# RWKV-7 mixer: the inverses of the 16x16 diagonal blocks by rows on GpSimd in place of doubling blocks on VectorE

## The chip, the cores and the metric

One core of a Trainium2 chip runs the whole program. The metric is the device time of one execution in microseconds (us), as the median of several runs. In the profile PE is the matrix engine, PEld its weight loads, DVE the vector engine, ACT the scalar engine, POOL the GpSimd engine, and SP the engine whose queue issues most DMAs.

## The reference, cut to what matters

A block of a streaming encoder: RMS norm, one input projection, two mixers side by side (a Mamba-2 state space mixer and an RWKV-7 mixer), an output projection, and a SwiGLU feed-forward layer. All is float32, 256 tokens of 2048 channels. The change lies in the RWKV-7 mixer, which the reference writes as a scan over tokens, for each of 32 heads of 64 channels:

```
def step(S, inp):
    r_t, w_t, k_t, v_t, a_t, b_t = inp
    sa = einsum('bhvk,bhk->bhv', S, a_t)
    S = S * w_t + sa[..., None] * b_t + v_t[..., None] * k_t
    return S, einsum('bhvk,bhk->bhv', S, r_t)
```

Taken by chunks of 64 tokens, the dependence of sa on earlier tokens of its own chunk is a strictly lower triangular 64x64 matrix N for each head and chunk, and the chunk needs the inverse of (I - N).

## The kernel before

**The stream.** The matrix products of the projections and of the feed-forward layer go through `gemm_a` and `gemm_b` in units: SP loads 512 KB of weights into `raw` (four buffers), ACT casts them to `whi` (L192), DVE computes the rest `wlo` (L193; four buffers each), and PE runs 24 matrix products of 256 columns (L277 to L279) or 12 of 512 (L298 to L300) on them. After each unit `side.tick()` traces the pieces of mixer work whose time has come.

**The RWKV mixer.** It is worked on in eight pairs of channel blocks, numbered 0 to 7 here: four heads and four chunks of 64 tokens each, thus 16 matrices N. A pair passes through three windows of the stream: its preparation (`PREP`), its matrices and their inverse (`AMATS`, `INV`), and the recurrence over its chunks (`CHAIN`: `step_r(c)` and `step_s(c)` for c from 0 to 3, then the group norm). So the inverse of pair k is computed in the window in which pair k-1 runs its recurrence. The numbers in the tables are ticks of a window, which has 16 of them, 12 for the first three.

**The inverse.** `amat("atb", ...)` computes N on PE and masks it on DVE. `inv_out` (L593 to L607) takes the four 16x16 diagonal blocks of each matrix out (`dg`, L602), and SP brings them over DRAM (`sc_n`, L604) into `nb` (L606), so that each of 64 partitions holds one block, `nb[i, t] = N[t, i]`. POOL sets `xb` to 64 identity matrices (L609, L610). `inv_level(s)` for s = 1, 2, 4, 8 then doubles the size of the inverted blocks in `xb`. Level 1 is a copy (L628). The others form two products for each pair of blocks, each as a DVE multiply into `pd` (L650) and a reduction (L652):

```
product(tv, n21.rearrange("p m j r -> p m r j"), x11)
product(x21, x22, tj)
```

`inv_in` (L658) transposes `xb` into `xbt` on DVE (L661), sends both over DRAM (`sc_X`, `sc_XT`, L664) back to tokens on the partitions (`cm`, L666), and spreads them into `XT` and `X` on DVE (L669). `lev16a` to `lev32b` (L686 to L723) go from 16 to 64 on PE (`ps_b`, L678). The result `XF` is first used in the next window.

**What else matters for the steps.** In the recurrence `step_s(c)` computes the new state `sn` on DVE (L766, L767), and `step_r(c+1)` reads it on PE (L736, into `ps_r`).

**Order.** Each engine works strictly through its own queue. Program order is set by the tables of ticks. The framework's scheduler then orders the instructions of each engine anew by a model of its own, except those that `keep_in_program_order` names, and sets semaphores for what depends on what. A DMA that waits in SP's queue holds up every DMA behind it.

Of the kernel before, what the change touches and what calls it, by code (L numbers as in the profile page):

```python
# [13 lines left out]
ALU = mybir.AluOpType  # L14
# [18 lines left out]
# ticks of a window at which the parts of three pairs of blocks are traced  # L33
# [8 lines left out]
class Side:  # L42
    """Work of the mixers, cut into small pieces that are traced between the pieces of the dense products."""
# [25 lines left out]
def tile_hybrid_block(ctx: ExitStack, tc: tile.TileContext, x, norm1_g, w_in, conv_w, conv_b, dt_bias, A_log, D_skip,  # L69
# [41 lines left out]
    # products that nothing reads: the tensor engine has its full clock only after a busy stretch  # L111
# [52 lines left out]
    # msk16: lower off-diagonal blocks on the way from 16 to 32 ([t, c])  # L164
# [35 lines left out]
    def square(i, pool, b, n, eng, order=lambda ins: ins):  # L200
        """the sum of squares of a quarter of each row"""
        src = h[:, b, n * 512:(n + 1) * 512]
        acc = ssq[i][:, b, n:n + 1]
        if eng == "act":
            order(nc.scalar.activation(pool.tile([P, 512], F32, name="sq_a"), src, AF.Square, accum_out=acc))
        else:
            order(nc.vector.scalar_tensor_tensor(pool.tile([P, 512], F32, name="sq_v"), src, 1.0, src, ALU.mult,
                                                 ALU.mult, accum_out=acc))
# [8 lines left out]
    def row_scale(i, pool):  # L217
        """one over the root mean square of each token, along the free dimension of every partition"""
        nonlocal R
        ps = mxt("ps_R")  # L220
        for b in range(2):
            r = finish(i, b)
            dg = pool.tile([P, P], F32, name="diag_r")
            nc.vector.tensor_scalar(dg, ident, r, None, ALU.mult)
            nc.tensor.matmul(ps[:, b * P:(b + 1) * P], ones, dg, start=True, stop=True)
        R = const.tile([P, T], F32, name="R")
        nc.scalar.copy(R, ps[:, :T])

    def scaled(ps):
        """a product of the raw rows becomes the one of the normalised rows"""  # L230
        nc.vector.tensor_tensor(ps, ps, R.unsqueeze(1).broadcast_to([P, 2, T]), ALU.mult)
        return ps

    def to_channels(n, gcol, order=lambda ins: ins):
        """a quarter of h times the norm's weight, with channels on the partitions; the rows' scale comes later"""
        nonlocal uh, ul
        if n == 0:
            uh = big.tile([P, KT, T], F32R, name="uh")
            ul = big.tile([P, KT, T], F32R, name="ul")
        tiles = []  # L240
        for k2 in range(2):
            ps = mxt("ps_n").rearrange("p (a t) -> p a t", a=2)
            tiles.append(ps)
            for b in range(2):
                for j in range(2):
                    c = n * 512 + (2 * k2 + j) * P
                    order(nc.tensor.transpose(out=ps[:, j, b * P:(b + 1) * P], in_=h[:, b, c:c + P], identity=ident))

        def half(k2):
            ks = [(4 * n + 2 * k2 + j, tiles[k2][:, j]) for j in range(2)]  # L250
            for k, ps in ks:
                order(nc.scalar.activation(uh[:, k], ps, AF.Copy, scale=gcol[:, k:k + 1]))
            for k, ps in ks:
                order(nc.vector.scalar_tensor_tensor(ul[:, k], ps, gcol[:, k:k + 1], uh[:, k].bitcast(F32), ALU.mult,
                                                     ALU.subtract))

        return half

    def load_a(w, cols, k0):
        """four row tiles of 256 columns; cols: [(place, width, column)]"""  # L260
        raw = wpool.tile([P, 4, 256], F32, name="raw", tag="raw", bufs=4)
        wv = w.rearrange("(k p) c -> p k c", p=P)
        for at, n, c in cols:
            nc.sync.dma_start(out=raw[:, :, at:at + n], in_=wv[:, k0:k0 + 4, c:c + n])
        return raw
# [17 lines left out]
    def gemm_b(w, r0, c0, acts, name):  # L283
        """acts: [(hi, lo)] with [P, T] each, one for a row tile of w; 512 columns"""
# [19 lines left out]
    def add_out(w, r0, ys, then=None):  # L304
        """ys: [(hi, lo)] of two row tiles each"""
# [9 lines left out]
    # the first product starts while x and its weights still come in, a quarter of the channels after the other  # L315
# [121 lines left out]
    def rwkv_pair(pi, st):  # L437
# [119 lines left out]
        def swap(dst, src, tmp):  # L557
            """the 64x64 blocks of src [(h c), (b c t)] transposed into dst [(h t), b c, c]"""
# [37 lines left out]
        # inverse of (I - N): blocks of 16 on one partition each, by halves of halves  # L596
        def inv_out():
# [7 lines left out]
            nb = tl("nb", (64, 272))  # L605
            nc.sync.dma_start(out=nb[:, :256].rearrange("p (i t) -> p i t", t=16),  # L606
                              in_=sc.rearrange("c (x i) t -> (c x) i t", i=16))  # L607
            xb = tl("xb", (64, 272))
# [4 lines left out]
        def inv_level(s):  # L613
            def f():
                nb, xb = st["nb"], st["xb"]
                nm = 8 // s

                def blocks(t, at, swap):
                    """block (row offset or column offset) of each of the nm diagonal blocks, [nm, s, s]"""
                    v = t[:, :nm * 34 * s].rearrange("p (m x) -> p m x", m=nm)[:, :, at:at + 16 * s]  # L620
                    v = v.rearrange("p m (j t) -> p m j t", t=16)[:, :, :, 0:s]
                    return v.rearrange("p m j t -> p m t j") if swap else v

                # nb is [i, t]: N[t, i]; xb is [t, c]
                n21 = blocks(nb, s, False)
                x11 = blocks(xb, 0, True)
                if s == 1:
                    nc.vector.tensor_copy(blocks(xb, 16, False), n21)  # L628
                    return
                x22 = blocks(xb, 17 * s, False)  # L630
                x21 = blocks(xb, 16 * s, False)
                tt = tl("tt", (64, 64), 2)
                # three free dimensions in an instruction: blocks of 2 by rows, larger ones by blocks
                if s == 2:
                    cut = [(slice(0, nm), r) for r in range(s)]
                    shp = [64, nm, s, s]
                    tv = tt[:, :nm * s * s].rearrange("p (r m c) -> p m r c", r=s, c=s)
                else:
                    cut = [(m, slice(0, s)) for m in range(nm)]
                    shp = [64, s, s, s]  # L640
                    tv = tt[:, :nm * s * s].rearrange("p (m r c) -> p m r c", r=s, c=s)
                tj = tv.rearrange("p m j c -> p m c j")

                def product(out, a, b):
                    """out[m, r, c] = sum over j of a[m, r, j] b[m, c, j]"""
                    for m, r in cut:
                        pd = tl("pd", (64, 512), 2, tag="t1")
                        pv = pd[:, :shp[1] * s * s].rearrange("p (a c j) -> p a c j", c=s, j=s)
                        bb = b[:, m] if s == 2 else b[:, m].unsqueeze(1)
                        nc.vector.tensor_tensor(pv, a[:, m, r].unsqueeze(2).broadcast_to(shp), bb.broadcast_to(shp),  # L650
                                                ALU.mult)
                        nc.vector.tensor_reduce(out[:, m, r], pv, axis=AX.X, op=ALU.add)  # L652

                product(tv, n21.rearrange("p m j r -> p m r j"), x11)
                product(x21, x22, tj)
            return f

        def inv_in():  # L658
            xbt = tl("xbt", (64, 16, 16), 2, tag="t1")
            xv = st["xb"][:, :256].rearrange("p (t c) -> p t c", c=16)  # L660
            nc.vector.tensor_copy(xbt, xv.rearrange("p t c -> p c t"))  # L661
# [12 lines left out]
        def blocks32(out, lhs, rhs, rows):  # L674
            """out[:, c] = lhs[:, c].T @ rhs[:, c] for 32x32 blocks; rows: [(input rows, output rows)]"""
            for c in range(NCH):
                for r, o in rows:
                    nc.tensor.matmul(out[o:o + 32, c], lhs[r:r + 32, c], rhs[r:r + 32, c], start=True, stop=True)  # L678
# [46 lines left out]
        # the chunks in their order  # L725
# [107 lines left out]
        inv = [inv_level(1), inv_level(2), inv_level(4), inv_level(8), inv_in, lev16a, lev16b, lev32a, lev32b]  # L833
# [239 lines left out]
    # the last 256 rows of w_down and the last norm, one half of the tokens after the other  # L1073
# [65 lines left out]
```

## Time and profile before

| what | value |
|---|---|
| time, median of 3 runs | 1697.96 us (1697.33 to 1699.16) |
| the profiled execution, from its first to its last instruction | 1697.0 us |
| PE busy | 1678.6 us, 99% |
| DVE busy | 1232.7 us, 73% |
| ACT busy | 892.1 us, 53% |
| POOL busy | 18.0 us, 1% |
| mean granted clock of PE | 0.998 |

The profile is of one execution. It gives the busy time of each engine, groups of instructions by line with their count, busy time and mean duration, the idle time ahead of them with the instruction that ended it, and a timeline with starts and durations. PE's products are pipelined: their spans overlap, so that a busy PE is not a PE at its peak. The windows of the eight pairs lie in the first 600 us, where DVE is busiest.

### The profile page before, as it was taken

The page shows a single profiled execution, that of the slowest core. Times are in us where ns is not written, and L with a number is a line of the kernel's source. Part 1 is how long each engine was busy: PE and PEld are TensorE (multiplying, and loading weights), DVE is VectorE, ACT ScalarE, POOL GpSimd, SP SyncE. Part 2 cuts the span into 40 slices and gives each one's busy share as a digit, 9 for nine tenths or more (in the row PEclk, how much of TensorE's full clock was granted, in tenths as well). Part 3 has the DMA queues.
Part 4 walks back from the last instruction along what each step waited for, and adds up shares of the span by engine and source line. Part 5 has one row for each costly group of instructions (what it writes and reads, how often), then busy time and mean ns, then how long its engine had stood idle before and what let it go on. Part 6 is the DMA issues. An engine that isn't in the chain of part 4 may idle for free.

```text
span 1697.0 us, 35291 instructions
## 1 busy us (share of the span) xinstructions
PE 1678.6 (99%) x14670; PEld 1546.5 (91%) x14670; DVE 1232.7 (73%) x1921; ACT 892.1 (53%) x1391; POOL 18.0 (1%) x57
## 2 busy tenths in 40 slices
PE   8999999999999999999999999999999999999997
PEld 8999989889898998998988999999999999999996
DVE  7998888989888868877768656556565565565657
ACT  6655665765646556666665543434434334344344
POOL 3000000000000000000000000000000000000000
PEclk9999999999999999999999999999999999999999
DMA  8554445544445456565554655555555555555553
GB/s 256 175 152 115 126 128 156 145 120 143 132 130 151 141 154 217 179 206 164 164 177 150 205 183 190 181 189 187 185 189 182 189 189 182 190 186 185 190 182 129
DMA packets 266720, 288.27 MB, mean 170 GB/s; under 512 B 43426, under 2 KB 216768, under 8 KB 265920
## 3 DMA queue, kind: packets, MB, share of 16 engines
q1 hardware_dynamic: 265232, 283.72, 54.0%
q8 instruction: 115, 1.88, 0.4%
q0 software_dynamic: 752, 1.24, 0.2%
q10 hardware_dynamic: 576, 1.05, 0.2%
q14 instruction: 45, 0.37, 0.1%
HBM read 282.27 MB, written 3.70 MB: 169 GB/s over the span
## 4 chain that ended last, share of the span: by engine, by line
PE 71%; DVE 2%; DMA 1%; ACT 1%; issue 0%; DVEq 0%
PE ps_o L298 7%; PE ps_o L300 7%; PE ps_o L299 7%; PE ps_up L279 5%; PE ps_up L277 5%; PE ps_up L278 5%; PE ps_gt L279 5%; PE ps_gt L278 5%; PE ps_gt L277 5%; PE ps_xs L277 2%; PE ps_xs L279 2%; PE ps_xs L278 2%; PE ps_z L300 2%; PE ps_z L298 2%; PE ps_z L299 2%; PE ps_bc L277 1%
## 5 line engine op out<-in xcount | busy, mean ns | idle before, releaser
L192 ACT CAST whi<-raw 128x1024 fp32r<-128x1024 f32 x508 | 532.2, 1048 | 655.2 <-PE ps_o L300 144.8
L193 DVE TENSOR_TENSOR wlo<-raw,whi 128x1024 fp32r<-128x1024 f32 x508 | 619.7, 1220 | 335.2 <-ACT whi L192 333.4
L277 PE MATMUL ps_rkv<-uh,whi 128*128 128x256 f32 x768 | 224.7, 293 | 0.0
L279 PE MATMUL ps_rkv<-uh,wlo 128*128 128x256 f32 x768 | 218.3, 284 | 0.7 <-DVE wlo L193 0.7
L278 PE MATMUL ps_rkv<-ul,whi 128*128 128x256 f32 x768 | 218.3, 284 | 0.0
L278 PE MATMUL ps_gt<-ul,whi 128*128 128x256 f32 x704 | 199.4, 283 | 0.0
L279 PE MATMUL ps_gt<-uh,wlo 128*128 128x256 f32 x704 | 199.3, 283 | 0.0
L277 PE MATMUL ps_up<-uh,whi 128*128 128x256 f32 x704 | 199.2, 283 | 0.0
L278 PE MATMUL ps_up<-ul,whi 128*128 128x256 f32 x704 | 199.2, 283 | 0.0
L279 PE MATMUL ps_up<-uh,wlo 128*128 128x256 f32 x704 | 199.2, 283 | 0.0
L277 PE MATMUL ps_gt<-uh,whi 128*128 128x256 f32 x704 | 199.2, 283 | 0.0
L277 PEld LDWEIGHTS ps_rkv<-uh,whi 128*128 128x128 f32 x768 | 146.7, 191 | 5.5 <-issue 1.4
L279 PEld LDWEIGHTS ps_rkv<-uh,wlo 128*128 128x128 f32 x768 | 146.7, 191 | 1.9 <-DVE wlo L193 1.1
L278 PEld LDWEIGHTS ps_rkv<-ul,whi 128*128 128x128 f32 x768 | 146.8, 191 | 0.6
L278 PEld LDWEIGHTS ps_gt<-ul,whi 128*128 128x128 f32 x704 | 135.1, 192 | 0.4
L277 PEld LDWEIGHTS ps_gt<-uh,whi 128*128 128x128 f32 x704 | 135.1, 192 | 0.4
L277 PEld LDWEIGHTS ps_up<-uh,whi 128*128 128x128 f32 x704 | 135.2, 192 | 0.0
L278 PEld LDWEIGHTS ps_up<-ul,whi 128*128 128x128 f32 x704 | 135.2, 192 | 0.0
L279 PEld LDWEIGHTS ps_up<-uh,wlo 128*128 128x128 f32 x704 | 135.2, 192 | 0.0
L279 PEld LDWEIGHTS ps_gt<-uh,wlo 128*128 128x128 f32 x704 | 135.1, 192 | 0.0
L298 PE MATMUL ps_o<-whi,ah 128*128 128x512 f32 x336 | 130.8, 389 | 0.0
L299 PE MATMUL ps_o<-wlo,ah 128*128 128x512 f32 x336 | 130.8, 389 | 0.0
(338 smaller groups left out, 3272.0 us busy)
## 6 DMA issues: line engine op xcount, KB each, us to landing
raw<-in_w_in_dram SPq DMA_DIRECT2D x180, 512.0 KB, 3.9
raw<-in_w_gate_dram SPq DMA_DIRECT2D x88, 512.0 KB, 3.6
raw<-in_w_up_dram SPq DMA_DIRECT2D x88, 512.0 KB, 3.5
raw<-in_w_down_dram SPq DMA_DIRECT2D x88, 512.0 KB, 3.6
raw<-in_w_out_dram SPq DMA_DIRECT2D x64, 512.0 KB, 3.9
csb<-cs_d SPq DMA_DIRECT2D x4, 1024.0 KB, 5.7
h<-in_x_dram SPq DMA_DIRECT2D x4, 512.0 KB, 7.8
g2s<-in_rwkv_g_dram SPq DMA_DIRECT2D x8, 256.0 KB, 3.3
```

The source lines that it names most:

```text
L192: order(nc.scalar.copy(hi, raw))
L193: order(nc.vector.tensor_tensor(lo, raw, hi.bitcast(F32), ALU.subtract))
L277: nc.tensor.matmul(o, wh, uh[:, kt], start=first and b == 0, stop=False)
L278: nc.tensor.matmul(o, wh, ul[:, kt], start=False, stop=False)
L279: nc.tensor.matmul(o, wl, uh[:, kt], start=False, stop=last and b == 1)
L298: nc.tensor.matmul(ps[b], ah[:, s], hi[:, k], start=first, stop=False)
L299: nc.tensor.matmul(ps[b], ah[:, s], lo[:, k], start=False, stop=False)
L300: nc.tensor.matmul(ps[b], al[:, s], hi[:, k], start=False, stop=last)
```

## The change

`inv_level` goes, and `inv_rows(i0, i1)` takes its place, four calls of four or three rows. It does forward substitution by rows: for i from 0 to 14, `N[t, i]` times row i of the inverse is added to all rows t below i. A step is a multiply into `pd` and an add into `xb`, both on GpSimd, on 64 partitions with 15 to 64 elements each; step 0 is a copy. Each step needs the one before. The transposed copy `xbt` is made on GpSimd as well, and lies in the buffer of `nb`. The ticks in `INV` stay as they are. For each pair DVE loses 22 instructions (a copy, ten multiplies, ten reductions, the transposing copy), and POOL gets 30 (two copies, 14 multiplies, 14 adds).

```diff
-            nb = tl("nb", (64, 272))
+            nb = tl("nb", (64, 256))
...
-            xb = tl("xb", (64, 272))
+            xb = tl("xb", (64, 256))
...
+        def inv_rows(i0, i1):
             def f():
+                nv = st["nb"][:, :256].rearrange("p (i t) -> p i t", t=16)
+                xv = st["xb"][:, :256].rearrange("p (t c) -> p t c", c=16)
+                for i in range(i0, i1):
+                    n, m = 15 - i, i + 1
+                    below = xv[:, m:, 0:m]
+                    if i == 0:
+                        nc.gpsimd.tensor_copy(below, nv[:, 0, 1:].unsqueeze(2))
+                        continue
+                    shp = [64, n, m]
+                    pd = tl("pd", (64, 64), 2)[:, :n * m].rearrange("p (t c) -> p t c", c=m)
+                    nc.gpsimd.tensor_tensor(pd, bc(nv[:, i, m:], m), xv[:, i, 0:m].unsqueeze(1).broadcast_to(shp),
+                                            ALU.mult)
+                    nc.gpsimd.tensor_tensor(below, below, pd, ALU.add)
             return f
...
-            xbt = tl("xbt", (64, 16, 16), 2, tag="t1")
+            xbt = tl("xbt", (64, 16, 16), tag="nb")
...
-            nc.vector.tensor_copy(xbt, xv.rearrange("p t c -> p c t"))
+            nc.gpsimd.tensor_copy(xbt, xv.rearrange("p t c -> p c t"))
...
-        inv = [inv_level(1), inv_level(2), inv_level(4), inv_level(8), inv_in, lev16a, lev16b, lev32a, lev32b]
+        inv = [inv_rows(0, 4), inv_rows(4, 8), inv_rows(8, 12), inv_rows(12, 15), inv_in, lev16a, lev16b, lev32a, lev32b]
```

The scheduler also sets other instructions in another order. Three places follow. Line numbers behind the changed function are 26 lower in the new file, and buffer numbers differ.

DVE in the window in which pair 2 is inverted, from the last state of the recurrence (`sn`) to `XT`, before:

```order
L767 TENSOR_TENSOR sn_3187<-sn_3187,pt_1153 128x128
L561 STREAM_TRANSPOSE ktt_3324<-kt_3061 128x512
L652 TENSOR_REDUCE xb_2895<-pd_3336 64x8x8
L354 SCALAR_TENSOR_TENSOR rkv_3218<-ps_rkv_2963,colA_161,rkv_3218 128x255
L661 COPY xbt_3339<-xb_2895 64x256
L193 TENSOR_TENSOR wlo_3386<-raw_3383,whi_3385 128x1024
L354 SCALAR_TENSOR_TENSOR rkv_3218<-ps_rkv_2963,colA_161,rkv_3218 128x255
L193 TENSOR_TENSOR wlo_3535<-raw_3532,whi_3534 128x1024
L560 STREAM_TRANSPOSE tmp2_3255<-rkv_3218 128x512
L746 TENSOR_TENSOR ws_3278<-ps_w_3273,nn_1898 128x128
L533 TENSOR_TENSOR ar_3727<-q_2994,pr_2785 128x8x64
L669 TENSOR_TENSOR XT_3345<-cm_3343,pmask_147 128x256
```

The same stretch of DVE's queue in the changed kernel, where L643 is `XT` and `X`, L740 and L741 are `sn`:

```order
L193 TENSOR_TENSOR wlo_3383<-raw_3380,whi_3382 128x1024
L515 TENSOR_TENSOR kt_3088<-kp_3013,pin_2806 128x512
L588 TENSOR_TENSOR atk_2946<-ps_a_3156,mask2_130 128x512
L643 TENSOR_TENSOR XT_3372<-cm_3370,pmask_147 128x256
L643 TENSOR_TENSOR X_3378<-cm_3376,pmask_147 128x256
L231 TENSOR_TENSOR ps_rkv_2981<-ps_rkv_2981,R_398 128x512
L561 STREAM_TRANSPOSE btt_3166<-bt_3086 128x512
L740 TENSOR_TENSOR sn_3213<-ps_s_3204,sn_3028 128x128
L354 SCALAR_TENSOR_TENSOR rkv_3243<-ps_rkv_2981,colA_161,rkv_3243 128x255
L741 TENSOR_TENSOR sn_3213<-sn_3213,pt_1162 128x128
L561 STREAM_TRANSPOSE ktt_3349<-kt_3088 128x512
L193 TENSOR_TENSOR wlo_3413<-raw_3410,whi_3412 128x1024
```

`XT` has moved ahead of two units' `wlo` and ahead of both `sn`. In all of pairs 2 to 7 it now stands ahead of that `sn`. PE's place for `ps_r<-sn` has not moved.

SP's queue in the same window, from the load of `nb`, before:

```order
L606 DMA nb_2893<-sc_n_2891 64x256
L290 DMA raw_3532<-in_w_out_dram 128x2x512
L290 DMA raw_3583<-in_w_out_dram 128x2x512
L290 DMA raw_3623<-in_w_out_dram 128x2x512
L664 DMA sc_X_3347<-xb_2895 64x256
L664 DMA sc_XT_3341<-xbt_3339 64x256
L290 DMA raw_3645<-in_w_out_dram 128x2x512
L666 DMA cm_3343<-sc_XT_3341 128x8x16
```

And in the changed kernel:

```order
L606 DMA nb_2911<-sc_n_2909 64x256
L290 DMA raw_3559<-in_w_out_dram 128x2x512
L638 DMA sc_X_3374<-xb_2913 64x256
L638 DMA sc_XT_3368<-xbt_3366 64x256
L290 DMA raw_3610<-in_w_out_dram 128x2x512
L640 DMA cm_3370<-sc_XT_3368 128x8x16
L640 DMA cm_3376<-sc_X_3374 128x8x16
L290 DMA raw_3650<-in_w_out_dram 128x2x512
```

`sc_X` has moved ahead of two loads of weights.

PE where pair 0's inverse is first used (`ps_b<-X`): before, in the units of `whi_1725` and `whi_1785`:

```order
L277 MATMUL ps_rkv_1506<-uh_182,whi_1725 128x256
L278 MATMUL ps_rkv_1506<-ul_183,whi_1725 128x256
L678 MATMUL ps_b_1545<-X_1498,atb_1214 32x32 x32
L279 MATMUL ps_rkv_1506<-uh_182,wlo_1726 128x256
L279 MATMUL ps_rkv_1782<-uh_182,wlo_1786 128x256
L277 MATMUL ps_rkv_1782<-uh_182,whi_1785 128x256
```

In the changed kernel:

```order
L278 MATMUL ps_rkv_1515<-ul_183,whi_1518 128x256
L279 MATMUL ps_rkv_1515<-uh_182,wlo_1519 128x256
L652 MATMUL ps_b_1554<-X_1507,atb_1214 32x32 x32
L277 MATMUL ps_rkv_1515<-uh_182,whi_1644 128x256
L278 MATMUL ps_rkv_1515<-ul_183,whi_1644 128x256
L279 MATMUL ps_rkv_1515<-uh_182,wlo_1645 128x256
```

PE meets pair 0's `X` 73 products of the stream sooner: ahead of the unit of `whi_1644`, which is `whi_1635` in the kernel before, its thirtieth unit. Pair 1's stands 31 products sooner, ahead of the forty-second unit. For pairs 2 to 7 PE has kept its order here.

More of the change, by code (lines that the diff above doesn't have):

```diff
@@ L611, in inv_out @@
             st["nb"], st["xb"] = nb, xb
-        def inv_level(s):
+        def inv_rows(i0, i1):
             def f():
[L615 to L655, printed above, removed]
```

## The prediction

> **What bounds the kernel now.** I read the page first, then PE's waits.
>
> ```profile
> PE 1678.6 (99%) x14670; PEld 1546.5 (91%) x14670; DVE 1232.7 (73%) x1921; ACT 892.1 (53%) x1391; POOL 18.0 (1%) x57
> ```
>
> ```profile
> PE ps_b L678 <- issue: 1.6, 1, 1.6
> PE ps_w L743 <- ACT rs L739: 0.8, 1, 0.8
> PE ps_b L678 <- DVE X L669: 0.7, 1, 0.7
> PE ps_rkv L279 <- DVE wlo L193: 0.7, 1, 0.7
> PE ps_b L678 <- DVE X L702: 0.4, 1, 0.4
> PE ps_b L678 <- DVE t1s L692: 0.3, 1, 0.3
> ```
>
> PE is the bound for the whole span. All that it waits for in the eight pairs' windows is these 4.5 us. So work taken off DVE can give back no more than these. Whatever makes PE wait, though, is added in full, because PE has no slack in which to catch up. Such a wait also costs something afterwards. Here are two stretches of 5 us behind the longest of the waits above; the last three columns are the granted clock of PE, the DMA share and GB/s:
>
> ```profile
> 440.00:445.00 5.00, 3.39 (x101) 2.37 (x89) 3.38 (x8) 4.00 (x11) 0.00 (x0) 0.90 0.46 130
> 445.00:450.00 5.00, 5.00 (x48) 4.19 (x48) 3.04 (x7) 4.90 (x12) 0.00 (x0) 0.76 0.00 0
> ```
>
> The clock falls to a mean of 0.90 and 0.76: 5 x 0.10 + 5 x 0.24 = 1.7 us of PE's time lost after a wait of 1.6 us.
>
> **What the change takes from DVE.** From the groups by line:
>
> ```profile
> L650 DVE TENSOR_TENSOR pd<-xb,tt 64x16 f32<-64x16 f32 (+2 forms) x40 | 14.2, 382 | 0.1
> L650 DVE TENSOR_TENSOR pd<-nb,xb 64x16 f32<-64x16 f32 (+2 forms) x40 | 13.6, 367 | 0.0
> ...
> L652 DVE TENSOR_REDUCE tt<-pd 64x8 f32<-64x16 f32 (+2 forms) x40 | 10.0, 277 | 0.2
> L652 DVE TENSOR_REDUCE xb<-pd 64x8 f32<-64x16 f32 (+2 forms) x40 | 9.8, 273 | 0.0
> ...
> L661 DVE COPY xbt<-xb 64x256 f32<-64x256 f32 x8 | 2.9, 363 | 0.0
> ...
> L628 DVE COPY xb<-nb 64x8 f32<-64x8 f32 x8 | 1.3, 160 | 2.7 <-DMA nb<-sc_n 2.7
> ```
>
> That is 51.8 us of DVE in all, 6.5 us a pair, beside PE's work. I credit the 4.5 us of waits and the 1.7 us of slow clock, 6.2 us, as the most that a lighter DVE can give.
>
> **How long there is for the new chain.** The inverse is a chain: `nb` lands, the blocks are inverted, `xbt` ends, the round trip over DRAM follows, then `XT` and `X`. Call C the time from the landing of `nb` to the end of `xbt`. DVE's timeline of pair 2 before:
>
> ```profile
> 205.63 0.17 DVE L628 COPY xb<-nb 64x8 f32<-64x8 f32 x1 [0.47 <-DMA nb<-sc_n]
> 205.72 0.68 DVE L513 TENSOR_TENSOR bt<-ta,pin 128x512 f32<-128x512 f32 x1
> ...
> 208.80 1.21 DVE L193 TENSOR_TENSOR wlo<-raw,whi 128x1024 fp32r<-128x1024 f32 x1
> ...
> 210.09 1.21 DVE L193 TENSOR_TENSOR wlo<-raw,whi 128x1024 fp32r<-128x1024 f32 x1
> ...
> 214.31 0.68 DVE L515 TENSOR_TENSOR kt<-kp,pin 128x512 f32<-128x512 f32 x1
> ...
> 216.54 1.21 DVE L193 TENSOR_TENSOR wlo<-raw,whi 128x1024 fp32r<-128x1024 f32 x1
> 217.68 0.70 DVE L561 STREAM_TRANSPOSE btt<-bt 128x512 f32<-128x512 f32 x1
> 218.31 0.24 DVE L766 TENSOR_TENSOR sn<-ps_s,sn 128x128 f32<-128x128 f32 x1
> 218.48 0.68 DVE L231 TENSOR_TENSOR ps_rkv<-ps_rkv,R 128x512 f32<-128x512 f32 x1
> 219.08 0.26 DVE L767 TENSOR_TENSOR sn<-sn,pt 128x128 f32<-128x128 f32 x1
> ...
> 220.88 0.48 DVE L354 SCALAR_TENSOR_TENSOR rkv<-ps_rkv,colA,rkv 128x255 f32<-128x255 f32 x1 [0.34 <-ACT rkv L353]
> 221.28 0.36 DVE L661 COPY xbt<-xb 64x256 f32<-64x256 f32 x1
> ...
> 227.55 0.43 DVE L669 TENSOR_TENSOR XT<-cm,pmask 128x256 f32<-128x256 f32 x1 [0.31 <-DMA cm<-sc_XT]
> 227.89 0.42 DVE L669 TENSOR_TENSOR X<-cm,pmask 128x256 f32<-128x256 f32 x1
> ```
>
> C is 16.0 us here (205.63 to 221.64), because the chain shares DVE with other work. From there to `XT` it is 5.9 us. Before the change both `sn` at 218.3 and 219.1 stand ahead of `XT`, so that the wait for `cm` keeps nobody. In the changed kernel they stand behind it: `XT`, `X`, L231, `btt`, `sn`, `rkv`, `sn`. Their durations add up to 3.2 us, and since each starts about 0.08 us ahead of its predecessor's end, they take 2.7 us. PE needs that `sn` at its old place, here for the pairs 2 and 6, with the landing for pair 6 and, in the last four rows, landing and first use for pairs 0 and 1:
>
> ```profile
> 221.39 0.28 PE L736 MATMUL ps_r<-sn,ar 64*64 64x64 f32 x4
> ...
> 482.88 0.17 DVE L628 COPY xb<-nb 64x8 f32<-64x8 f32 x1 [1.30 <-DMA nb<-sc_n]
> ...
> 497.81 0.28 PE L736 MATMUL ps_r<-sn,ar 64*64 64x64 f32 x4
> ...
> 98.45 0.16 DVE L628 COPY xb<-nb 64x8 f32<-64x8 f32 x1
> ...
> 108.87 0.28 PE L277 MATMUL ps_rkv<-uh,whi 128*128 128x256 f32 x1
> ...
> 149.61 0.12 DVE L628 COPY xb<-nb 64x8 f32<-64x8 f32 x1
> ...
> 165.71 0.28 PE L277 MATMUL ps_rkv<-uh,whi 128*128 128x256 f32 x1
> ```
>
> - Pairs 2 to 7: 221.39 - 205.63 = 15.8 us, less 5.9 and 2.7, leaves C at most 7.2 us; for pair 6, 14.9 us leaves 6.3. I take 6.75 for all six, 40.5 in all.
> - Pair 0: PE now meets `X` ahead of the unit that began at 108.87. 10.4 us, less 5.9, less 1.2 for `XT`, `rkv` and `X`, leaves 3.3.
> - Pair 1: ahead of the unit that began at 165.71. 16.1 us, less 5.9 and 0.8, leaves 9.4.
>
> Together 53.2 us. If C is the same for all pairs and above 9.4, PE waits 8C - 53.2 us more. If it is smaller, pair 1 drops out first.
>
> Behind the blocked `XT` stand also two units' `wlo` (PE uses the first some 8 us after `ps_r`, and DVE needs 2 us for it after `sn`). Behind SP's blocked `sc_X` stand loads of weights, which in the kernel before were issued some 10 us earlier but not used for 20 us. I cost both at nothing; the four buffers hide them, up to a delay of about 6 us.
>
> **How long the new chain takes.** No arithmetic runs on POOL before. The nearest rows:
>
> ```profile
> L609 POOL MEMSET xb<- 64x272 f32 x8 | 2.5, 318 | 265.6 <-DMA sc_X<-xb 265.6
> L155 POOL TENSOR_SCALAR_AFFINE_SELECT mask<-mask 64x64 f32<-64x64 f32 x4 | 1.3, 357 | 0.0
> L610 POOL MEMSET xb<- 64x16 f32 x8 | 1.0, 119 | 0.5
> ```
>
> L610 waits for L609 as each step here waits for the last: 0.5 us idle over 8, 0.06 us each. A step is then no less than 0.119 + 0.06 = 0.18 us (it also reads two operands, and has 47 elements on the mean). The nearest row that reads and writes 64x64 gives 0.357 + 0.06 = 0.42 us. I take 0.34, nearer the second, since the second also reads: 28 x 0.34 = 9.5, 0.2 for the first copy, and 0.8 for `xbt` (256 elements a partition, between 0.32 for the memset of that size and four times 0.357): 10.5 us.
>
> DVE may add to it. While the chain runs, DVE has five instructions that read two operands from SBUF: 0.68, 0.68 and three `wlo` of 1.21, 5.0 us. Whether they hold up POOL no row before can show, since POOL there only writes. I take half, 2.5. So C = 13.0 us, with bounds of 28 x 0.18 + 0.2 + 0.4 = 5.6 and 28 x 0.42 + 0.2 + 1.4 + 5.0 = 18.4.
>
> [...]
>
> **The sum.** PE waits 8 x 13.0 - 53.2 = 50.8 us more. Each of the eight waits, of 3.6 to 9.7 us, is longer than the one that cost 1.7 us of clock, so 8 x 1.7 = 13.6 us. [...] Credit: 6.2 us. Net 58.2, on the profiled 1697.0: 1755.2 us. The median of the runs shown is 0.9 us above the profiled span, so **1756 us**.
>
> **The rivals.**
>
> 1. *DVE and POOL block one another in full.* The 5.0 us then count whole: C = 15.5 and 8 x 15.5 - 53.2 = 70.8, plus 13.6, less 6.2: 1776 us. [...] Against the full price: DVE is stuck at `XT` early and then holds nothing.
> 2. *A short chain, small waits.* At 0.22 to 0.27 us a step C is near 8.5. Pair 1 does not wait; the other seven wait 7 x 8.5 - 43.8 = 15.7 us, 11.9 us of clock, less 6.2: 1719 us. For it: the memset's 0.18.
> 3. *Faster.* The one mechanism is that the chain comes off DVE's path altogether: with C up to 6.75, a step below 0.2 us, `XT` finds `cm` landed, `sn` is in time, and only pair 0 waits, 2.3 to 3.5 us, with or without 1.7 us of clock. Against that stand 6.2 us of credit, so 1694 to 1697 us. For it: before, the chain's own work on DVE is 6.5 us a pair and stretches to 16 for company; alone on POOL it has none. Against it: a step would have to run like a memset of 16 elements.
>
> **How the numbers follow.** A difference of 0.2%, 3.4 us, is about what a measurement of this kernel can tell. My forecast (C between 10 and 14.5) gets 0.60, rival 1 gets 0.22, rival 2 gets 0.12, rival 3 gets 0.06. All but the last are slower, and a little of rival 2 and half of the last are no change: slower 0.93, same 0.04, faster 0.03. The range reaches from C = 7.6 (six waits of 0.9 and one of 4.3 us, some 5 us of clock, less 6.2: 1706) to C = 18.4 (94.0 + 13.6 - 6.2 = 101, 1799, and some clock beyond one slow stretch for waits of over 10 us: 1805).
>
> **What would show it.** Right: a new wait of PE at `ps_r` (L710) for DVE's `sn` (L741), six times, each 4 to 9 us; PE waiting for DVE's `X` at `ps_b` for pairs 0 and 1; `XT` with a long idle ahead of it put down to `cm<-sc_XT`; POOL busy for 80 to 100 us more; DVE 52 us less; granted clock below 1 in the slices from 100 to 570 us. Wrong: steps of POOL under 0.2 us; PE without waits at `ps_r`; or a span that grows elsewhere, as in the feed-forward layer, which has no pairs.

## The result, and the profile after

The changed kernel takes 1787.34 us (median of 4 runs, 1784.93 to 1790.22), the kernel before in the same comparison 1697.86 us (1697.33 to 1699.16): a ratio of 1.0528, 95% interval 1.0513 to 1.0543. The forecast was 1756 us. The profiled execution spans 1788.5 us, 91.5 us more than before.

The page of the changed kernel, busy times and the row of the granted clock by slices:

```profile
PE 1708.2 (96%) x14670; PEld 1574.9 (88%) x14670; DVE 1192.5 (67%) x1745; ACT 892.0 (50%) x1391; POOL 110.4 (6%) x297
...
PEclk9989889898989989999999999999999999999999
```

POOL works 92 us more, DVE 40 us less. (DVE's 176 removed instructions add up to 51.8 us by groups, but each overlaps with its neighbours on DVE; in the trace before, DVE without them is busy 39 us less.) The clock row was all nines before; now seven of its first fifteen slices show an eight, and it is whole again from slice 16 on, where the pairs are through.

PE's waits after (total us, times, longest):

```profile
PE ps_r L710 <- DVE sn L741: 38.8, 6, 7.2
PE ps_b L652 <- DVE X L643: 15.6, 2, 10.4
PE ps_rkv L279 <- DVE wlo L193: 8.7, 4, 2.4
...
PE ps_bc L279 <- DVE wlo L193: 2.1, 1, 2.1
PE ps_b L652 <- DVE t1s L666: 1.6, 1, 1.6
```

The first two rows are the waits that were forecast, at their places and in their numbers: six at `ps_r`, two at `ps_b`, 54.4 us. The `wlo` rows are five waits that no step of the prediction had, and neither is the one for `t1s`, which follows at once on the wait for `X` at pair 1.

DVE's timeline of pair 2, and further down the place of one of those five waits:

```profile
227.38 1.23 DVE L193 TENSOR_TENSOR wlo<-raw,whi 128x1024 fp32r<-128x1024 f32 x1
...
230.46 1.23 DVE L193 TENSOR_TENSOR wlo<-raw,whi 128x1024 fp32r<-128x1024 f32 x1 [0.52 <-ACT whi L192]
...
236.57 0.68 DVE L588 TENSOR_TENSOR atk<-ps_a,mask 128x512 f32<-128x512 f32 x1
246.09 0.42 DVE L643 TENSOR_TENSOR XT<-cm,pmask 128x256 f32<-128x256 f32 x1 [8.84 <-DMA cm<-sc_XT]
...
248.62 0.28 DVE L741 TENSOR_TENSOR sn<-sn,pt 128x128 f32<-128x128 f32 x1
...
282.85 0.69 DVE L803 TENSOR_TENSOR yl<-yc,yh 128x512 fp32r<-128x512 f32 x1 [1.84 <-ACT yh L802]
283.45 0.68 DVE L534 TENSOR_TENSOR ar<-rkv,pr 128x512 f32<-128x512 f32 x1
284.06 1.22 DVE L193 TENSOR_TENSOR wlo<-raw,whi 128x1024 fp32r<-128x1024 f32 x1
```

DVE reaches `XT` at 237 and stands there 8.84 us until `cm` has landed, and the `sn` that PE wants stand behind it. Forty microseconds later DVE stands 1.84 us before `yl`, which waits for ACT's `yh`, with the next `wlo` behind it. Before the change the order at that place was `yc`, `ar`, `wlo`, `yl`, and `yl` waited for nothing:

```profile
250.55 0.68 DVE L534 TENSOR_TENSOR ar<-rkv,pr 128x512 f32<-128x512 f32 x1
251.15 1.22 DVE L193 TENSOR_TENSOR wlo<-raw,whi 128x1024 fp32r<-128x1024 f32 x1
252.30 0.69 DVE L829 TENSOR_TENSOR yl<-yc,yh 128x512 fp32r<-128x512 f32 x1
```

The scheduler has put `yl` two places earlier.

POOL's timeline of the chain of pair 2, and the groups by line that belong to it:

```profile
226.54 0.36 POOL L623 COPY xb<-nb 64x15 f32<-64x15 f32 x1 [17.95 <-DMA nb<-sc_n]
...
227.60 1.11 POOL L627 TENSOR_TENSOR pd<-nb,xb 64x39 f32<-64x39 f32 x1
...
230.54 1.29 POOL L627 TENSOR_TENSOR pd<-nb,xb 64x60 f32<-64x60 f32 x1
...
239.47 0.21 POOL L629 TENSOR_TENSOR xb<-xb,pd 64x15 f32<-64x15 f32 x1
239.74 0.61 POOL L635 COPY xbt<-xb 64x256 f32<-64x256 f32 x1
```

```profile
L627 POOL TENSOR_TENSOR pd<-nb,xb 64x28 f32<-64x28 f32 (+3 forms) x112 | 44.0, 393 | 8.8
L629 POOL TENSOR_TENSOR xb<-xb,pd 64x28 f32<-64x28 f32 (+3 forms) x112 | 39.6, 353 | 8.8
L635 POOL COPY xbt<-xb 64x256 f32<-64x256 f32 x8 | 4.9, 614 | 0.5
L623 POOL COPY xb<-nb 64x15 f32<-64x15 f32 x8 | 3.9, 489 | 216.2 <-DMA nb<-sc_n 216.2
```

A step takes 0.373 us on the mean and has 0.079 us of idle ahead (8.8 / 112). C is 28 x 0.452 + 0.49 + 0.61 = 13.8 us, and so it is in the timeline (226.5 to 240.35).

PE's windows of 5 us around that pair's wait (length, PE busy and its count, granted clock, DMA share, GB/s):

```profile
240.00:245.00 5.00, 2.43 (x23) 0.97 0.65 147
245.00:250.00 5.00, 1.04 (x13) 0.50 0.44 115
250.00:255.00 5.00, 4.92 (x27) 0.50 0.48 132
```

PE gets its data at 249 and then runs at half clock until 255. Between the first 30 us and the last microseconds the trace has 13 such stretches, 105.8 us in all. PE is idle in 31.9 of these, so (105.8 - 31.9) x 0.5 = 36.9 us of its work were lost to the clock, against 1.7 us before.

### The profile page after: what moved, and what is told of

Same layout as the page of the kernel before. It is cut to its first block, busy times and chain, and to the rows that moved or that the text cites. A ratio compares the mean times of both kernels' runs of the same rounds, so it can differ in the third digit from the quotient of the medians.

```text
span 1788.5 us, 35328 instructions
## 1 busy us (share of the span) xinstructions
PE 1708.2 (96%) x14670; PEld 1574.9 (88%) x14670; DVE 1192.5 (67%) x1745; ACT 892.0 (50%) x1391; POOL 110.4 (6%) x297
## 4 chain that ended last, share of the span: by engine, by line
PE 63%; DVE 0%; ACT 0%; DVEq 0%; issue 0%
PE ps_o L298 7%; PE ps_o L300 7%; PE ps_o L299 7%; PE ps_up L279 5%; PE ps_up L278 5%; PE ps_up L277 5%; PE ps_gt L279 5%; PE ps_gt L278 5%; PE ps_gt L277 5%; PE ps_xs L277 2%; PE ps_xs L279 2%; PE ps_xs L278 2%; PE ps_z L300 2%; PE ps_z L298 2%; PE ps_z L299 2%; PE ps_yd L928 1%
## 5 line engine op out<-in xcount | busy, mean ns | idle before, releaser
L279 PE MATMUL ps_rkv<-uh,wlo 128*128 128x256 f32 x768 | 226.6, 295 | 8.7 <-DVE wlo L193 8.7
L277 PE MATMUL ps_rkv<-uh,whi 128*128 128x256 f32 x768 | 234.8, 306 | 0.0
L278 PE MATMUL ps_rkv<-ul,whi 128*128 128x256 f32 x768 | 226.3, 295 | 0.0
L279 PEld LDWEIGHTS ps_rkv<-uh,wlo 128*128 128x128 f32 x768 | 155.8, 203 | 9.4 <-DVE wlo L193 9.2
L277 PEld LDWEIGHTS ps_rkv<-uh,whi 128*128 128x128 f32 x768 | 155.2, 202 | 6.2 <-issue 1.4
L278 PEld LDWEIGHTS ps_rkv<-ul,whi 128*128 128x128 f32 x768 | 155.9, 203 | 0.5
```

Source lines behind the costliest of these rows:

```text
L277: nc.tensor.matmul(o, wh, uh[:, kt], start=first and b == 0, stop=False)
L278: nc.tensor.matmul(o, wh, ul[:, kt], start=False, stop=False)
L279: nc.tensor.matmul(o, wl, uh[:, kt], start=False, stop=last and b == 1)
```

## The experiments

**The theory ("queue").** Nothing is wrong with the work on GpSimd itself. DVE's queue is in order, and an instruction in it that waits for the longer chain (`XT`, then `X`; 8.84 us before `XT` of pair 2) holds up what PE needs next. Each such wait then costs clock as well. **The rivals:** the work on GpSimd takes the time by blocking DVE; or the chain of many small steps is too long on any engine. With each result stand two sums from its trace: how long PE was idle from 30 us on until its last product, and what the half-clock stretches in that time cost PE beside that. (Of pin_spread's 28.8 us, 2.9 belong to a stretch at 30.5 us, ahead of the first pair's inverse.) Less the kernel before's 5.0 and 1.7, they should give the difference in span, and do within some 11%. Each ratio is to runs of the kernel before on the same chip:

| kernel | median us | ratio to before, 95% interval | PE idle | clock lost | span more than before |
|---|---|---|---|---|---|
| before | 1697.86 | 1 | 5.0 | 1.7 | 0 |
| changed | 1787.34 | 1.0528 (1.0513 to 1.0543) | 67.4 | 36.9 | 91.5 |
| pin_spread | 1768.14 | 1.0413 (1.0398 to 1.0429) | 55.3 | 28.8 | 73.0 |
| spread_late | 1759.49 | 1.0359 (1.0343 to 1.0374) | 31.0 | 40.6 | 62.1 |
| spread_pool | 1731.51 | 1.0196 (1.0170 to 1.0221) | 29.8 | 14.9 | 34.7 |
| rows7 | 1757.27 | 1.0340 (1.0325 to 1.0356) | 40.6 | 29.8 | 59.3 |
| yl_later | 1775.49 | 1.0441 (1.0422 to 1.0459) | 60.9 | 27.2 | 77.6 |
| all_moved | 1704.84 | 1.0032 (1.0021 to 1.0042) | 8.5 | 7.6 | 8.8 |
| pool_load | 1702.56 | 1.0021 (1.0012 to 1.0030) | 10.3 | 1.6 | 5.5 |
| rows_on_dve | 1712.98 | 1.0079 (1.0063 to 1.0094) | 14.6 | 8.5 | 16.2 |
| all_moved_2 | 1709.88 | 1.0082 (1.0068 to 1.0096) | 9.8 | 9.3 | 11.2 |
| clock_dose | 1786.04 (one run) | | 72.9 | 17.6 | 87.2 |
| hybrid | 1695.31 | 0.9981 (0.9972 to 0.9990) | 2.7 | 0.0 | -3.6 |

**pin_spread: only the order of `XT` and `sn`.**

```diff
-                nc.vector.tensor_tensor(dst.rearrange("p c (b t) -> p c b t", t=16),
+                pin(nc.vector.tensor_tensor(dst.rearrange("p c (b t) -> p c b t", t=16),
...
```

> Only the place of XT and X in DVE's queue changes: for the pairs 2 to 6 they move behind the two sn (they then stand 2 instructions behind the second sn, and the next unit's wlo 3 behind XT); pairs 0, 1 and 7 stay as they are. Theory 'sn': the six waits at ps_r are the whole harm of pairs 2 to 6, so five of them (33.3 us) and their clock (about 17 us) go: 1735 to 1740 us. Theory 'queue': DVE still stands before XT until cm has landed, and PE then waits about as long for the wlo that is now next behind it; 5 to 7 us each, put down to wlo and no longer to sn: 1770 to 1790 us. Theory 'POOL itself is the cost': 1787 us.

1768.14 us. PE's waits:

```profile
PE ps_y L751 <- DVE ws L720: 22.1, 5, 6.2
PE ps_b L652 <- DVE X L643: 15.7, 2, 10.2
PE ps_r L710 <- DVE sn L741: 6.1, 1, 6.1
```

The five waits for `sn` are gone, the sixth, in pair 7 where nothing moved, stays; and in place of the five PE now waits five times for `ws`, the next thing that it wants from a DVE that stands before `XT`. The theory "sn" falls. "Queue" holds, with another victim than the `wlo` that I had named, shorter waits (3.6 to 6.2 us) and a time 2 us below its range. The waits for `wlo` behind `yl` are shorter here as well (7.5 us instead of 10.8), and only the longest of them, of 1.74 us, is followed by a half-clock stretch.

**spread_late: `XT` where `cm` has landed.**

```diff
-INV = (5.002, 6.276, 7.732, 9.62, 9.939, 11.691, 11.849, 12.652, 15.9)
+INV = (5.002, 6.276, 7.732, 9.62, 9.939, 12.9, 14.1, 14.3, 15.0, 15.9)
...
+        def inv_spread():
+            for key in ("XT", "X"):
...
+                pin(nc.vector.tensor_tensor(dst.rearrange("p c (b t) -> p c b t", t=16),
...
-        inv = [..., inv_in, lev16a, lev16b, lev32a, lev32b]
+        inv = [..., inv_in, inv_spread, lev16a, lev16b, lev32a, lev32b]
```

> The spreading of cm into XT and X is traced 3 ticks (about 15 us) later and the four steps to 64 accordingly, so that DVE reaches XT after cm has landed; the chain on GpSimd stays. Theory 'queue': with C still at 13 to 14.5 us, no wait of PE of over 1 us for pairs 2 to 7, at most one for pairs 0 or 1, granted clock back at 0.99: 1690 to 1702 us. Theory 'POOL and DVE block one another' (the chain itself costs): the time stays at 1770 to 1787 us.

1759.49 us: a miss. The wait that it was made against is gone: no wait at `ps_r` is left, and `XT` of pair 2 starts at 266.54 with no idle ahead. But the steps from 16 to 64 now follow one another within half a unit, and PE waits between them. The longest of these waits, of 4.0, 4.5 and 5.4 us, lie at the pairs 0 and 1, where DVE still stands 9.8 and 7.8 us before `XT`. Waits, and windows of PE in pair 2:

```profile
PE ps_b L656 <- DVE t1s L670: 9.9, 2, 5.4
PE ps_b L656 <- DVE X L647: 9.7, 6, 4.0
```

```profile
265.00:270.00 5.00, 3.12 (x113) 1.00 0.14 33
270.00:275.00 5.00, 4.16 (x84) 0.52 0.36 93
```

Two waits of 1.15 and 0.7 us among 128 products of 32x32 come ahead of a stretch of 13.7 us at half clock, from 270.2 on; a third wait of 0.8 us and more such products lie within it. In the pairs 2 to 6 the clock cost 3.0 to 6.4 us each, more than the waits. So this run doesn't say that the chain harms; it says that my new place was bad.

**spread_pool: DVE out of the chain.**

```diff
-                nc.vector.tensor_tensor(dst.rearrange("p c (b t) -> p c b t", t=16),
+                nc.gpsimd.tensor_tensor(dst.rearrange("p c (b t) -> p c b t", t=16),
```

> XT and X are computed on GpSimd, at the old ticks, so that DVE never waits for cm. Theory 'queue': the waits of pairs 2 to 7 at ps_r (38.8 us) and at wlo (10.8 us) go; PE meets X for pairs 0 and 1 as early as in the changed kernel, so 10 and 5 us stay there and perhaps 1 us more since GpSimd is slower at it, with about 10 us of clock: 1715 to 1730 us. Theory 'POOL and DVE block one another': more work on GpSimd, so no better than 1787 us.

1731.51 us, 1.5 us above the range of "queue" and 56 us less than the changed kernel, with more work on GpSimd. PE's waits:

```profile
PE ps_b L652 <- POOL X L643: 17.3, 2, 10.9
PE ps_rkv L279 <- DVE wlo L193: 10.2, 4, 3.2
...
PE ps_bc L279 <- DVE wlo L193: 2.2, 1, 2.2
```

All waits for `sn` are gone; C is as long as ever (224.6 to 238.5 in pair 2). The rival "POOL and DVE block one another" would have had it no better than 1787 us. What I had wrong: the five waits for `wlo` stay. They have nothing to do with the wait before `XT`.

**rows7: a shorter chain, rows 0 to 6 alone.**

```diff
-                for i in range(i0, i1):
+                for i in range(i0, min(i1, 7)):
```

> Only rows 0 to 6 of the substitution are done, 12 multiplies and adds in place of 28 (rows 7 to 14 are left out, so the inverse is incomplete); XT still stands ahead of sn in DVE's queue. C should come to 5.5 to 7 us, at the edge of the 6.75 us that the pairs 2 to 7 were said to have. Theory 'queue': waits at ps_r of 0 to 0.5 us each, pair 0 still waits about 3 us, 1694 to 1706 us. Theory 'the cost goes with the work on GpSimd': 12/28 of 90 us stay, 1735 us.

1757.27 us, above the ranges of both theories: another miss. C is 7.2 us (214.7 to 221.9 in pair 2). PE's waits:

```profile
PE ps_r L710 <- DVE sn L741: 16.1, 6, 3.6
PE ps_rkv L279 <- DVE wlo L193: 9.2, 4, 3.0
PE ps_w L717 <- ACT rs L713: 5.8, 6, 1.4
```

The waits at `ps_r` fell from 6.5 to 2.7 us each, so they do follow the length of the chain. They did not fall to nearly nothing: my margin of 6.75 us is some 2 us too wide for this kernel, in which `XT` stands 7 instructions ahead of the first `sn` and not 4. The clock fell only from 36.9 to 29.8 us: what a wait costs in clock depends little on its length. And the waits for `wlo` stay here too. In pair 1, `XT` has come to stand ahead of `ws`, and PE waits 4.7 us for that `ws`: the same mechanism at one more place. Why PE also waits 5.8 us for ACT's `rs` stays open.

**yl_later: the waits for `wlo`.** DVE's order at the end of a window, with the changed kernel's rows ahead of this kernel's:

```
L798 yc<-ps_g,yc   L311 h<-ps_o,h x2   L803 yl<-yc,yh   L534 ar<-rkv,pr   L193 wlo<-raw,whi
L799 yc<-ps_g,yc   L312 h<-ps_o,h x2   L535 ar<-rkv,pr   L194 wlo<-raw,whi   (yl further down)
```

```diff
-            nc.vector.tensor_tensor(yl, yo, yh.bitcast(F32), ALU.subtract)
+            st["y"] = yo, yh, yl
+        def final_low():
+            yo, yh, yl = st["y"]
+            pin(nc.vector.tensor_tensor(yl, yo, yh.bitcast(F32), ALU.subtract))
...
+        if 2 < pi < 10:
+            side.at(1.3, pairs[pi - 3]["low"])
```

> The changed kernel, with one DVE instruction traced later: the low part yl of the RWKV output, which now stands in DVE's queue ahead of ar and the next unit's wlo and waits 1.85 us there for ACT's yh, goes behind them, as it did before the change. Theory 'new order': the second wave of PE's waits, for wlo some 40 us after each of the pairs 2 to 6 (2.1 to 2.4 us each, 10.8 in all), and its five half-clock stretches (about 9 us lost) have nothing to do with GpSimd; they go: 1765 to 1770 us, and the waits at ps_r stay at 6 to 7 us each. Theory 'the wave is an echo of the wait before XT': no change, 1784 to 1790 us.

1775.49 us, 11.9 less than the changed kernel. The first row of PE's waits:

```profile
PE ps_r L711 <- DVE sn L742: 40.4, 6, 7.4
```

No wait of PE for `wlo` is left, and the five half-clock stretches behind them are gone. The waits for `sn` stay. It gave less than the 17 to 22 us that I expected; the traces of the two differ by 13.9 us in span, and by 16.2 in the two sums.

**pool_load: GpSimd's work where nobody waits for it.**

```diff
+                    for i in range(1, 15):
+                        n, m = 15 - i, i + 1
...
+                        nc.gpsimd.tensor_tensor(pd, bc(nv[:, i, m:], m), ...
+                        nc.gpsimd.tensor_tensor(x3, x3, pd, ALU.add)
                     nc.vector.tensor_copy(blocks(xb, 16, False), n21)
```

> The kernel before, with 28 multiplies and adds of the sizes of the substitution on GpSimd for each pair, on data of their own, that start when nb lands and whose result nothing reads; every other engine keeps its order. It measures what the work on GpSimd costs DVE where nobody waits for it. Theory 'queue': a few DVE instructions lose 0.1 to 0.2 us each, hidden: 1696 to 1701 us. Theory 'POOL and DVE block one another': DVE loses up to 5 us in each pair in a place where PE's lead is short: 1710 to 1740 us. For GpSimd: steps of 0.25 to 0.30 us alone and over 1 us where a wlo runs.

1702.56 us, 0.21% (0.12 to 0.30%) or some 4 us above the kernel before. The steps on POOL, and PE's longest row of waits:

```profile
L637 POOL TENSOR_TENSOR x<-x,pd 64x28 f32<-64x28 f32 (+3 forms) x112 | 65.6, 586 | 8.8
L635 POOL TENSOR_TENSOR pd<-nb,x 64x28 f32<-64x28 f32 (+3 forms) x112 | 63.0, 562 | 207.0 <-DMA nb<-sc_n 198.9
```

```profile
PE ps_w L753 <- ACT rs L749: 4.3, 5, 1.7
```

Beside a DVE that is doubling blocks, a step takes 0.57 us instead of 0.37. DVE pays little: by the pages it is busy 1236.8 us against 1232.7. So the steps on GpSimd do run slower beside DVE's work, by 0.20 us each, while DVE has 4.1 us more in all. By itself the work costs the kernel some 4 us, not 90.

**rows_on_dve: the algorithm without the move.**

```diff
-                        nc.gpsimd.tensor_copy(below, nv[:, 0, 1:].unsqueeze(2))
+                        nc.vector.tensor_copy(below, nv[:, 0, 1:].unsqueeze(2))
...
```

> The same forward substitution with its 30 instructions on DVE, GpSimd back to where it was: the algorithm without the move. The scheduler then places XT 22 to 25 instructions behind sn again. DVE gets 28 steps of 0.1 to 0.25 us for 20 multiplies and reductions of 0.3 us, 4 to 7 us a pair instead of 6.5, in a chain. Theory 'order and latency': no wait at ps_r; 1694 to 1712 us. Theory 'the longer chain of small steps is the harm, on whichever engine': PE waits at ps_b for X as C grows past 20 us: over 1730 us.

1712.98 us, just outside what I expected. The steps, on DVE:

```profile
L627 DVE TENSOR_TENSOR pd<-nb,xb 64x28 f32<-64x28 f32 (+3 forms) x112 | 21.4, 191 | 1.5
L629 DVE TENSOR_TENSOR xb<-xb,pd 64x28 f32<-64x28 f32 (+3 forms) x112 | 21.2, 189 | 1.6
```

Half as long as in the changed kernel, but with other work between them C of pair 2 is 19.9 us (210.5 to 230.4), and PE waits for `X` six times, 8.2 us in all. Yet the kernel is only 0.8% slower than before: with a longer C than on GpSimd it loses a sixth of what the changed kernel loses, and `XT` stands behind `sn` here. A long chain alone doesn't cost 90 us. `yl` stands ahead of `ar` and `wlo` here too, but waits only 0.1 to 0.2 us for `yh`, and the four waits for `wlo` are 1.8 us in all: the new order costs much only where `yh` is late.

**all_moved: all three places together.** `XT` and `X` on GpSimd, `yl` as in yl_later, and the steps from 16 to 64 of the pairs 0 and 1 later:

```diff
+INV12 = ((11.1, 11.2, 11.3, 11.9), (10.1, 10.3, 11.1, 11.9))
...
+                if pi < 3 and j > 4:
+                    t = INV12[pi - 1][j - 5] * 16 / (ticks - 0.5)
```

> Forward substitution stays on GpSimd as in the changed kernel. XT and X on GpSimd, yl behind the next wlo, and for pairs 0 and 1 the steps from 16 to 64 traced 2 to 3 units later. Theory 'queue': nothing in DVE's queue waits for the chain any more and PE reaches ps_b after X in every pair, so the 33 us that were left with XT and X on GpSimd go, and DVE is 8 us a pair lighter than before the change: 1691 to 1699 us. Theory 'POOL and DVE block one another': the longer GpSimd works, the more DVE loses; not below 1715 us.

1704.84 us, 0.32% above the kernel before: 83 us of the loss are gone with the substitution still on GpSimd and C at 14 to 16 us. It is 6 us above the range of "queue", and 10 below that of the rival. Most of what is left lies at the pairs 0 (4.7 us of waiting for `X`, 2.5 of clock) and 1 (a wait of 1.6 us that the trace puts down to issue, and 5.1 of clock).

**all_moved_2: pairs 0 and 1 earlier.**

```diff
-                side.at(t, f)
+                side.at(t * 0.5 if pi < 3 else t, f)
```

> As all_moved, but the matrices of the pairs 0 and 1 are traced earlier (half the tick), which brings nb about 5 us earlier, and the steps from 16 to 64 of pair 1 start one unit earlier, so that they lie further apart. What all_moved still lost was 4.7 us of waiting and 2.5 us of clock at pair 0 and 1.6 and 5.1 us at pair 1. Theory 'queue': at least 8 of these 14 us go: 1691 to 1699 us. If they come back as new waits elsewhere in these two windows: 1701 to 1706 us.

1709.88 us, worse. `nb` of pair 0 came only 0.9 us earlier (97.4 instead of 98.3 us). PE waits there 3.8 us for `X` and 3.3 us for `t1s`, and the clock costs 9.3 us. SP's and ACT's timelines of that place:

```profile
113.29 0.50 SPq L640 DMA_DIRECT2D sc_X<-xb  x1
```

```profile
118.52 1.04 ACT L194 CAST whi<-raw 128x1024 fp32r<-128x1024 f32 x1 [10.38 <-DMA raw<-in_w_in_dram]
```

SP issues nothing from 96.5 to 113 us, until the chain gives `sc_X` its data; the loads of weights stand behind it, and ACT is without work for 10.38 us. DVE then has four `wlo` to do ahead of `t1s`. A better place for the chain in the 12-unit windows I did not find.

**clock_dose: the price of a bare wait.** The kernel before, in ten places of the feed-forward layer:

```diff
+                d = fp.tile([P, P], F32, name="dd", bufs=1)
+                nc.gpsimd.tensor_copy(d, sg[:, 0, :P])
+                for _ in range(DOSE[j]):
+                    nc.gpsimd.memset(d, 0.0)
+                pin(nc.tensor.matmul(mxt("ps_d")[:, :P], ones, d, start=True, stop=True))
```

> The kernel before, with ten waits put into the feed-forward layer, where PE otherwise never waits: a product that nothing uses reads a tile that GpSimd writes 36 to 100 times over, and the next unit stays behind it. By the memsets of the profile (0.26 us with the gap) the waits should be about 0, 1, 2, 3, 4, 5.5, 7, 9, 12 and 16 us, 60 us in all; the steps on GpSimd meet DVE's wlo, but write only. It measures what a wait costs in clock, apart from the mixers. As forecast (1.7 us for each wait): 14 us of clock, 1772 us. Theory 'a wait of more than about 1 us brings two to four stretches of 3.4 us at half clock, whatever its length': 3 to 5 us for each, 25 to 40 us of clock, 1783 to 1797 us.

1786.04 us. PE's waits, and windows of PE at the wait of 6.2 us:

```profile
PE ps_d L1078 <- POOL dd L1077: 67.3, 10, 17.2
```

```profile
1305.00:1310.00 5.00, 0.00 (x0) 0.72 0.62 200
1310.00:1315.00 5.00, 4.67 (x25) 0.59 0.00 0
```

The time came into the range of the theory (a clock loss of 3 to 5 us for each wait) not because of the clock: the waits were longer than I had reckoned (67.3 us for 60), and some 3 us of the longer span are in neither of the two sums. Waits of 1.3 and 1.4 us cost no clock. The other eight, of 2.5 to 17.2 us, cost 1.5, 1.7, 2.8, 1.9, 2.3, 1.4, 2.8 and 1.5 us, 2.0 on the mean, whatever their length. For a wait amid full-sized products the forecast's 1.7 us were about right, and "3 to 5 us each" falls.

What PE does after a wait seems to matter. In the changed kernel's trace the half-clock stretches of the pairs' windows begin and end on a grid of 3.41 us: they last one to four such steps (3.41 to 13.65 us), and the full-clock stretches between them 9 to 16 (30.72 to 54.61 us). So one can ask of each step of this grid at half clock how busy PE was in it, and whether the full clock came back at its end. Here is one step of clock_dose, with full-sized products alone:

```profile
1467.69:1471.10 3.41, 2.87 (x13) 0.50 0.00 0
```

PE was busy for 84% of it, and the full clock came back. In the next two PE was busier, and the clock stayed at a half for one step more: the first, of the changed kernel, holds 64x64 products of the recurrence, and the second, of all_moved, holds 32x32 products of an inverse:

```profile
412.00:415.41 3.41, 3.34 (x26) 0.50 0.28 86
```

```profile
188.60:192.02 3.42, 3.42 (x44) 0.50 0.00 0
```

Small products don't always keep the clock down: the changed kernel's step at 493.9 us has 64x64 products too and was as busy as that at 412.0, and the clock came back behind it.

**hybrid: rows on GpSimd only where there is time.** Pairs 2 to 7 as in all_moved, pairs 0 and 1 as before the change:

```diff
+        if pi < 2:
+            inv[:4] = [inv_level(s) for s in (1, 2, 4, 8)]
```

> Pairs 0 and 1, whose inverse is needed within a window of 12 units, as before the change: doubling on DVE, XT and X on DVE, at the old places. Pairs 2 to 7 as in all_moved: rows, XT and X on GpSimd, yl behind the next wlo. PE's waits and half-clock stretches of all_moved lay at the pairs 0 and 1 (6.3 us of waiting, 7.6 of clock) and nearly nowhere else. Theory 'queue': PE waits less than 5 us in all after the start, 1692 to 1696 us, thus 1 to 5 us below the kernel before, which is all that PE waited there. If DVE in these windows is then the bound again, or GpSimd's part costs PE something that is no wait: 1697 to 1703 us.

1695.31 us, some 3 us (0.10 to 0.28%) below the kernel before, and so the shortest time of all: small, but clear of the noise. Page and PE's longest wait for another engine in the pairs' windows:

```profile
PE 1675.5 (99%) x14670; PEld 1544.7 (91%) x14670; DVE 1196.8 (71%) x1777; ACT 891.7 (53%) x1391; POOL 96.4 (6%) x249
```

```profile
PE ps_rkv L280 <- DVE wlo L194: 0.8, 1, 0.8
```

PE has 2.7 us of idle left after the start, and DVE is 36 us lighter than before, which is worth next to nothing, as PE is the bound.

## Why the prediction was right, and where its sizes were off

- **The path: right.** DVE's queue stands before `XT`, and PE waits for the `sn` behind it. pin_spread moved the victim, spread_pool removed the wait at the same C, rows7 shortened it with C.
- **C: 13.0 forecast, 13.8 measured.** Without `wlo` beside it a step lasts 0.281 us (189 of the 224), with the gap 0.36, forecast 0.34; the first copy and `xbt` take 1.1 us (1.0); and the steps beside a `wlo` add 28 x (0.373 - 0.281) = 2.6 us (2.5). The forecast of half the price of DVE's company was a choice between two values that nothing before could settle, and it came out by luck.
- **PE's waits: 8C - 53.2 = 50.8 forecast; 54.4 measured.** With C = 13.8 the formula gives 57.2, so that C a little too short and margins a little too narrow have in part cancelled. By place: 6.5 us at `ps_r` (13.8 - 6.75 = 7.05), 10.4 at pair 0 (13.7 - 3.3 = 10.4), 5.3 at pair 1 (14.3 - 9.4 = 4.9).
- **The credit of 6.2 us: taken.** Of the 5.0 us of idle of the kernel before 0.6 are left, and its clock loss is gone.
- **The `wlo` behind the blocked `XT`, costed at nothing: held, but another term was missed.** For those `wlo` no wait shows. But 10.8 us of waits for `wlo` come from `yl` ahead of `ar` and `wlo`: a change of order some 40 us from the place of the change. yl_later shows it, and prices it with its clock at 11.9 us by the medians (13.9 by the traces). The order of the changed kernel had it; I had looked only around `XT`.
- **Loads behind SP's `sc_X`, costed at nothing: held.** In the changed kernel PE's only wait at pair 0 is the one for `X`, and in the pairs 2 to 7 of all_moved, with C at 14 us, no wait comes from them. It is near its limit at pair 0: in all_moved_2 ACT ran dry there, and PE's 3.3 us for `t1s` came behind the late `wlo`.
- **The clock: the mis-sized term.** "Each of the eight waits, of 3.6 to 9.7 us, is longer than the one that cost 1.7 us of clock, so 8 x 1.7 = 13.6 us." In yl_later the eight half-clock stretches are those of the eight waits, and they cost 27.2 us: 3.4 each. (At pair 1 a further wait of 1.6 us lies within the stretch.) clock_dose shows that 2.0 is the price where full-sized products follow: its wait of 6.2 us cost 1.9 us of clock, while the changed kernel's six at `ps_r`, of 5.5 to 7.2 us, cost 2.2 to 3.7. Inside the mixers' windows it is nearly twice that. That the small products of the recurrence hold the clock down longer would fit the steps of the grid shown at clock_dose (still at a half behind 64x64 products at 98% busy, full again behind full-sized ones at 84%), but the step at 493.9 us does not fit, and no run took them away from behind a wait: it stays a reading.
- **The sum.** 62.4 us more idle and 35.2 us more clock make 97.6, the span grew by 91.5. The count of clock by halves takes all of PE's busy time as bound by its clock, so it is an upper end; by the span less the idle, 29 to 35 us is what the clock cost, where 13.6 less the credited 1.7 were forecast.
- **Rival 1** was right that DVE's work holds up GpSimd's; the other way round the trace shows next to nothing. Beside the `wlo` of 227.38 and 230.46 two steps take 1.11 and 1.29 us that take 0.25 and 0.28 (at 237.92 and 558.07) where DVE is idle, and the 35 steps that meet a `wlo` last 0.87 us on the mean. `wlo` hardly notices: 1.229 us with a step beside it, 1.221 without. The price was half of the rival's. Its 1776 us lie nearer to the result than the forecast, but by accident: its C of 15.5 is not what the chain took, and the rest is the clock and `yl`. **Rival 2** fell with the step's price. **Rival 3**, a faster kernel, exists, but by order and not by a short chain: hybrid.

## What to carry to other kernels

Before a chain is moved to a slower engine, look at what stands in in-order queues behind the instruction that consumes it. Here 83 of the 90 us were gone once that instruction had left the queue, the first uses at the pairs 0 and 1 stood later and `yl` stood behind the next `wlo` (12 us of the 90); the new engine's work as such cost some 4. Move the consumer, or its waiting, off the queue that feeds the bound engine, and compare the whole order, not only the place of the change: the scheduler can set instructions anew some 40 us away. A wait of the bound engine costs its length and a piece of clock that in clock_dose hardly depended on the length (1.4 to 2.8 us of it for waits of 2.5 to 17.2 us), so that several waits of that kind cost more than one of the same sum.

## What the runs showed of the hardware

- The half-clock stretches of the changed kernel from 30 us on last 3.41, 6.83, 10.24 and 13.65 us, multiples of 3.41. In clock_dose the clock fell at a wait of 2.5 us and not at 1.3 or 1.4; in the kernel before it fell behind one of 1.6 us.
- PE was not always idle for the whole step of that grid: in the step ahead of each of the 13 falls of the changed kernel from 30 us on it was busy 0 to 48%, and in nine of them above 0. In the last step of each of these stretches it was busy 98 to 100%, in the one of clock_dose at 1467.69 us 84%, and the full clock came back. With small products in the step the clock stayed at a half behind one busy 98% (the changed kernel's at 412.00 us) and one busy 100% (all_moved's at 188.60 us).
- In the changed kernel the slowing was one-sided: a step on GpSimd took 0.28 us without a `wlo` beside it and 0.87 with one, a `wlo` on DVE 1.221 us without a step beside it and 1.229 with one.
- A dependent multiply or add of 15 to 64 elements a partition takes 0.35 us from start to start on GpSimd where DVE is idle beside it (the changed kernel's trace); on DVE one of 15 or 28 elements takes 0.20 to 0.22 where two follow one another directly (rows_on_dve's, from 229.23 us on).
